# Interleaving the first two MLP products by pair, an end without GpSimd, and adaLN sums in program order, in a hybrid GLA / DeltaNet block

## The chip, the cores and the metric

The kernel runs on one core of a Trainium2 chip. A core has TensorE (PE, with its weight loads shown as PEld), VectorE (DVE), ScalarE (ACT), GpSimd (POOL) and SyncE (SP). Each engine works through its own instructions in order, and semaphores join the engines. Data lie in HBM, in SBUF (128 partitions) and in PSUM, where TensorE writes its results. Most transfers are issued by SP, in the order of its queue, and some by ACT.

The metric is the time of one execution on the device, in microseconds (us). The profile is of one execution; its span runs from the first to the last instruction.

## The reference

One residual block for a sequence of 1024 tokens and a model width of 1024, all in float32. `c` is a conditioning vector. In short:

```
mod = silu(c) @ ada_w + ada_b                 # 6 x 1024: shift1 scale1 gate1 shift2 scale2 gate2
h   = rms_norm(x, pre_mix_w) * (1 + scale1) + shift1
proj = h @ w_in                               # q, k, v, gates of both branches
o_a = gla_chunked(...)                        # gated linear attention, 4 heads, chunks of 64
o_d = gated_delta_chunked(...)                # gated delta rule, 8 heads, chunks of 64
merged = sigmoid(m_a) * (o_a @ w_branch_gla) + sigmoid(m_d) * (o_d @ w_branch_gdn)
x  = x + gate1 * rms_norm(merged @ w_out, post_mix_w)
h2 = rms_norm(x, pre_mlp_w) * (1 + scale2) + shift2
y  = square(relu(h2 @ mlp_w1)) @ mlp_w2       # D_FF = 4096
x  = x + gate2 * rms_norm(y, post_mlp_w)
```

The delta branch needs, for each head, a decay matrix `exp(gc_i - gc_j)` below the diagonal, with `gc` the running sum of the log gates.

## The kernel before

**Numbers.** Each matrix product takes three passes: an operand is split into a high part (an ACT cast) and a low part (a DVE subtraction), and high x high, high x low and low x high are summed in PSUM.

**Order of the work.** The first part of the program, up to the `flush()` in line 1250, leaves the order on each engine to a planner, which places instructions by their dependencies, their place in the program and its own estimates of time. `tc.issue_after(ins)` adds an order without a wait: what is traced inside comes later than `ins` on the engine of `ins`. A counter of ticks spreads work along the matrix products: `at(dt, fn)` (line 328) traces `fn` when `dt` more ticks have gone by (an entry that is due runs at the next tick), and `tick()` is called after every group of matmuls (of a dense tile's eight k steps, each one; of a product of the MLP's first layer, two). From line 1254 on, the token stage and the MLP, the class `InOrder` (line 27) chains every instruction of PE, DVE, ACT, POOL and SP behind the one traced before it on that engine: there the order is the program's.

**Stages by time in the profile.** To about 100 us: loads, norms, the first part of adaLN. About 100 to 210 us: the key tiles of the delta branch (`dense_b` in line 395, eight ticks for a tile; `conv` in line 560 reads a tile's PSUM, one ACT pass and three DVE passes; PSUM holds two such tiles). In it `gdn_D` (line 640) loads `gr`, at tick 4 `decay` (line 632) makes eight DVE instructions and an exponential of it, at tick 10 it is stored. Then the branch gates and a triangular solve on DVE, the GLA heads (`gla_head`), the delta heads (`gdn_head`, to about 1100 us), the branch products, and the token stage (eight tiles of 128 tokens: `merged @ w_out`, norm, residual, second norm, transposes `tr`, lines 1279 to 1315), to about 1370 us.

**The rest of adaLN.** Four of the six parts of `mod` are summed on DVE along the GLA and delta heads: `ada_rest(n)` (line 1078), called at tick 2 + 13 n for n from 0 to 31, loads a block `araw` of 128 rows on SP into one of two `sl` buffers, and eight ticks later `ada_sum` (line 1085) adds it to `aacc`. After each eighth, `ada_total` three ticks later (line 1094) sums over the partitions with TensorE and makes the column `gcol` on DVE, and two ticks after that `ada_row` (line 1109) transposes `gcol` on TensorE.

**The MLP.** The two matrix products are done by a Strassen-Winograd scheme with seven products on 2 x 2 blocks. The hidden width is cut into 16 pairs g. *Pass 1* (lines 1475 to 1501) makes for each pair the product with block B11 (12 matmuls into a bank), copies the bank out with ACT (`uy[:, 0]`, stored to `u_d`), then goes on in the same bank with B21 (12 matmuls), and ACT takes relu and square (`uy[:, 1]`, stored to `y_d`). Weights come as `raw`, 512 KB for a pair; `prep_pass1` makes the high and low parts of one product. `t_ops` are the block differences T1 to T4 and their splits (19 steps) for *pass 2*, which does the other five products of each pair (lines 1642 to 1669) with weights from `prep_pass2`. `uy` lies in the two `sl` buffers, which the token stage uses for `xr` just before. Then comes the second layer (line 1736 on), whose last chunk is done token tile by token tile (line 1804 on), each followed by `finish` (line 1767): add the tile to `yacc` on DVE, square sum on ACT, product with the gate on GpSimd, an inverse root on DVE for that tile (13 small instructions), and one tile later a scaling on ACT and the last addition on GpSimd, and the store. In the last tile the halves are done apart.

Of the kernel before, what the change touches and what calls it, by code (L numbers as in the profile page):

```python
# [26 lines left out]
class InOrder:  # L27


    def __init__(self, tc, engine):  # L30
        self.tc, self.engine, self.strict, self.last = tc, engine, False, None

    def __getattr__(self, name):
        fn = getattr(self.engine, name)
        if not self.strict:
            return fn

        def call(*args, **kw):
            with self.tc.issue_after(self.last) if self.last else nullcontext():
                r = fn(*args, **kw)  # L40
            self.last = r.ins
            return r
        return call


@with_exitstack
def block_kernel(ctx: ExitStack, tc: tile.TileContext, x, c, ada_w, ada_b, pre_mix_w, post_mix_w,
# [1030 lines left out]
    def ada_rest(n):  # L1078
# [3 lines left out]
        DMA.dma_start(raw, ada_w[k * 128:(k + 1) * 128, ADA[i][0]:ADA[i][0] + 1024])  # L1082
        at(8, lambda: ada_sum(i, k, raw))

    def ada_sum(i, k, raw):
        if k == 0:
            adat[i] = t4(p="aacc", tag="hd")
            V.tensor_scalar(adat[i], raw, sc[:, k:k + 1], None, ALU.mult)
        else:
            V.scalar_tensor_tensor(adat[i], raw, sc[:, k:k + 1], adat[i], ALU.mult, ALU.add)  # L1090
        if k == 7:
            at(3, lambda: ada_total(i))

    def ada_total(i):
# [4 lines left out]
        if dst is None:  # L1099
# [3 lines left out]
            at(2, lambda: ada_row(i, g))  # L1103
# [175 lines left out]
    def token_chain(t, ps, xr):  # L1279
# [79 lines left out]
    raw1 = {}  # L1359

    def load_pass1(g):

        r_ = rp.tile([128, 8, 2, 128], F32, tag="raw", name=nm("raw"))
        for i in range(2):
            LD.dma_start(r_[:, :, i, :], mlp_w1[:, (g + i) * 256:(g + i) * 256 + 128].rearrange("(k p) c -> p k c", p=128))
            raw1[g + i] = r_[:, :, i, :]
# [14 lines left out]
    for t in range(NT):  # L1381
# [12 lines left out]
        if t == 7:
            prep_pass1(0, 0, 3)
            prep_pass1(0, 1, 4)
            at(6, lambda: split_op("B21", F[0][2:4], (1,)))
# [77 lines left out]
    at(12, lambda: todo.extend(t_ops()))  # L1475
    for g in range(NG):
        ps = pat()
        uy = pair_tile("uy", "sl")
        if g % 2 == 0:
            at(3, lambda g=g: load_pass1(g + 4) if g + 4 < NG else load_pass2((g + 4 - NG) // 2))  # L1480
        if g + 1 < NG:
            if g:
                prep_pass1(g + 1, 0, 0)
            prep_pass1(g + 1, 1, 1)
        if g == NG - 2:
            todo += prep_pass2(0)
        if g == NG - 1:
            load_uy(0)
        for j in (1, 3) if g < NG - 2 else range(4):
            at(j, lambda: some(1))  # L1490
# [6 lines left out]
        def store(g=g, uy=uy):  # L1497
            LD.dma_start(u_d[g], uy[:, 0])
            LD.dma_start(y_d[g // 2][0, :, g % 2, :], uy[:, 1])

        at(2, store)
# [345 lines left out]
```

## Time and profile before

| | us |
|---|---|
| median of 3 runs (2037.9 to 2039.47) | 2039.18 |
| the profiled execution: time | 2040.46 |
| the profiled execution: span | 2038.7 |
| ACT busy in it | 786.3 |
| POOL busy in it | 214.7 |
| mean granted TensorE clock (1 is full) | 0.983 |

The views used below: the *page* has busy times of the engines; the *windows* give busy time, number of instructions and granted clock (PEclk) in stretches of the span; the *waits* say which engine stood for whom (in all, times, longest); the *timeline* has instructions in order of time, merged where they are alike, with the idle time before them in square brackets; the *chain* is the work that ended last, followed back from the end. `<-` stands between what is written and what is read, or between an engine and the one that released it. L40 is the line in `InOrder` that all instructions of the strict part have, so there one goes by the tiles' names. L365 is a dense tile's matmul.

### The profile page before, as it was taken

Reading aid. Unit: us, or ns where it says so; the run is one execution under the profiler, and the core shown is the slowest. Engines: PE = TensorE matmul, PEld = TensorE weight load, DVE = VectorE, ACT = ScalarE, POOL = GpSimd, SP = SyncE. Lnnn points to the kernel's source line nnn. Section 1 sums busy time; section 2 is a strip of 40 time slices with the busy share of each in tenths; the row PEclk is TensorE's granted clock in tenths of the full one; section 3 lists DMA queues with packets and bytes.
Section 4 is the critical chain, followed back from the end, with each engine's and each line's share of the span. In section 5 each row is a group of like instructions: output and inputs, shape, how many; then the busy total and the mean of one; then the engine's idle time right before and its main releaser. Section 6 shows DMA issues by size and latency. Waiting matters only on the chain.

```text
span 2038.7 us, 26028 instructions
## 1 busy us (share of the span) xinstructions
PE 1943.1 (95%) x9894; PEld 1628.7 (80%) x9894; DVE 1469.8 (72%) x2642; ACT 786.3 (39%) x1410; POOL 214.7 (11%) x131
## 2 busy tenths in 40 slices
PE   6999999999899999999999999998899999999995
PEld 4777888989799878888887888876688888888884
DVE  7757699568658697778777455664478886777877
ACT  5544323243242333333434121354544546433332
POOL 4300100310110100000002121000011110000015
PEclk8899999999899999999999999998999999999998
DMA  9356632213211343233435342334567777353334
GB/s 298 114 207 223 215 104 83 94 52 125 62 53 54 105 158 101 91 92 110 132 109 179 123 143 93 107 100 135 165 207 227 242 226 263 136 206 115 133 114 145
DMA packets 198797, 287.52 MB, mean 141 GB/s; under 512 B 33536, under 2 KB 137423, under 8 KB 198671
## 3 DMA queue, kind: packets, MB, share of 16 engines
q1 hardware_dynamic: 176910, 250.84, 37.9%
q10 hardware_dynamic: 21760, 35.01, 4.8%
q8 instruction: 78, 1.28, 0.3%
q14 instruction: 49, 0.39, 0.1%
HBM read 210.70 MB, written 75.11 MB: 140 GB/s over the span
## 4 chain that ended last, share of the span: by engine, by line
PE 70%; DVE 18%; ACT 5%; DMA 5%; issue 2%; SPq 0%; POOL 0%; DVEq 0%; ACTq 0%; POOLq 0%
PE pm L365 30%; PE pa L40 20%; PE pm L40 9%; DVE obT L587 4%; DMA araw<-in_ada_w_dram 2%; DVE rt L40 2%; PE pm L984 1%; DVE cv L564 1%; PE pm L986 1%; PE pm L985 1%; DVE rs L40 1%; DVE wL L351 1%; PE pa L778 1%; ACT uy L40 1%; DVE xr L40 1%
## 5 line engine op out<-in xcount | busy, mean ns | idle before, releaser
L365 PE MATMUL pm<-hH,wH 128*128 128x512 f32 x1008 | 330.4, 408 | 7.1 <-DVE cv L564 7.1
L365 PE MATMUL pm<-hH,wL 128*128 128x512 f32 x1008 | 314.0, 392 | 1.6 <-DVE wL L351 1.6
L365 PE MATMUL pm<-hL,wH 128*128 128x512 f32 x1008 | 314.7, 393 | 0.0
L365 PEld LDWEIGHTS pm<-hH,wL 128*128 128x128 f32 x1008 | 190.1, 189 | 43.8 <-DVE wL L351 2.0
L365 PEld LDWEIGHTS pm<-hL,wH 128*128 128x128 f32 x1008 | 190.5, 189 | 41.7
L40 PE MATMUL pa<-w,yH 128*128 128x512 f32 x688 | 212.0, 389 | 0.0
L350 ACT CAST wH<-raw 128x1024 fp32r<-128x1024 f32 x95 | 99.1, 1052 | 287.9 <-PE pm L365 203.8
L365 PEld LDWEIGHTS pm<-hH,wH 128*128 128x128 f32 x1008 | 177.2, 191 | 33.5 <-issue 5.0
L40 DVE TENSOR_TENSOR w<-raw,w 128x512 fp32r<-128x512 f32 (+1 forms) x142 | 122.1, 873 | 81.9 <-ACT w L40 81.4
L40 PEld LDWEIGHTS pa<-w,yH 128*128 128x128 f32 x688 | 129.1, 188 | 27.1 <-DVE ya L40 0.4
L40 PE MATMUL pa<-oB,w 128*128 128x512 f32 x480 | 120.8, 407 | 19.6 <-ACT uy L40 19.6
L40 PE MATMUL pa<-w,yL 128*128 128x512 f32 x344 | 133.8, 389 | 0.0
L40 ACT CAST w<-raw 128x512 fp32r<-128x512 f32 (+1 forms) x143 | 96.9, 710 | 87.6 <-DVE raw L40 82.3
L40 PEld LDWEIGHTS pa<-oB,w 128*128 128x128 f32 x480 | 92.0, 195 | 45.5 <-ACT uy L40 26.4
L351 POOL TENSOR_TENSOR wL<-raw,wH 128x1024 fp32r<-128x1024 f32 x27 | 66.3, 2459 | 582.3 <-ACT wH L350 562.1
L564 DVE SCALAR_TENSOR_TENSOR cv<-pm,ccol,cv 128x1023 f32<-128x1023 f32 (+2 forms) x72 | 92.1, 1279 | 20.0 <-ACT cv L562 19.1
L351 DVE TENSOR_TENSOR wL<-raw,wH 128x1024 fp32r<-128x1024 f32 x68 | 83.6, 1236 | 27.8 <-ACT wH L350 26.2
L40 PE MATMUL pm<-oT,w 128*128 128x512 f32 x384 | 90.8, 389 | 0.0
L40 PE MATMUL pa<-oT,w 128*128 128x512 f32 x384 | 90.8, 389 | 0.0
L40 DVE TENSOR_TENSOR ya<-pa,ya 128x512 f32<-128x512 f32 x82 | 55.8, 690 | 43.7 <-PE pa L40 43.6
L40 PEld LDWEIGHTS pa<-oT,w 128*128 128x128 f32 x384 | 72.1, 188 | 15.0
L40 PEld LDWEIGHTS pm<-oT,w 128*128 128x128 f32 x384 | 72.1, 188 | 15.0
(368 smaller groups left out, 3932.9 us busy)
## 6 DMA issues: line engine op xcount, KB each, us to landing
yL<-y_d SPq DMA_DIRECT2D x53, 512.0 KB, 8.6
raw<-in_mlp_w_dram SPq DMA_DIRECT2D x24, 1024.0 KB, 5.7
raw<-in_w_in_dram SPq DMA_DIRECT2D x19, 1024.0 KB, 5.3
raw<-in_w_in_dram SPq DMA_DIRECT2D x34, 512.0 KB, 4.5
araw<-in_ada_w_dram SPq DMA_DIRECT2D x32, 512.0 KB, 3.8
araw<-in_ada_w_dram SPq DMA_DIRECT2D x32, 256.0 KB, 6.3
sg_d<-sig ACTq DMA_DIRECT2D x16, 512.0 KB, 6.4
sl<-sg_d SPq DMA_DIRECT2D x16, 512.0 KB, 4.5
```

Of the source, the lines that this page charges most:

```text
L40: r = fn(*args, **kw)
L350: A.copy(wH, raw_ap)
L351: E.tensor_tensor(wL, raw_ap, wH.bitcast(F32), ALU.subtract)
L365: last["pe"] = T.matmul(ps[:, hf * 512:(hf + 1) * 512], wt[:, k, :], rhs(k, hf, lo), start=(k == 0 and wt is wH and lo == 0), stop=(k == 7 ...
L564: last["ev"] = V.scalar_tensor_tensor(y[:, s:], ps[:, :S - s], ccol[:, (3 - s) * 24 + ct:(3 - s) * 24 + ct + 1], y[:, s:], ALU.mult, ALU.a ...
L587: V.transpose(dst[b:b + 32, :, a:a + 32], src[a:a + 32, :, b:b + 32])
L778: T.matmul(pt[:, i * 128:(i + 1) * 128], kT[:, sl], q[:, sl], start=True, stop=True)
L984: T.matmul(pp, hH[k][:, tok], wh[:, k % 4, :], start=(k == 0), stop=False)
L985: T.matmul(pp, hH[k][:, tok], wl[:, k % 4, :], start=False, stop=False)
L986: last["pe"] = T.matmul(pp, hL[k][:, tok], wh[:, k % 4, :], start=False, stop=(k == 7)).ins
```

## The change

- `InOrder` now remembers the last instruction of its engine (`recent`) in the planned part too. `V.behind()` puts what is traced inside it behind the last DVE instruction traced so far. `decay` and `ada_sum` are traced in it. `decay` is due at tick 8 for head 0 (4 for the others), its store at 12.
- The load of `araw` comes behind the last weight load of the program on SP. `ada_total` comes 8 ticks after the last sum (3 before), `ada_row` 10 ticks after that (2 before).
- The transposes `tr` of the token stage come one tick later.
- Pass 1 goes through the products in the order (0,0), (1,0), (0,1), (2,0), (1,1), ...: between the two products of a pair lie the second of the pair before and the first of the pair after. Parts of the weights are made two products ahead. Two fixed buffers hold `raw`, loaded pair by pair. `uy` lies in `w4` buffers for g below 4 and from 10 on, and in the `sl` buffers for the others; its two halves are stored one by one. Pass 2's weights are loaded one pair further ahead, and those of its first two pairs are made within pass 1.
- At the end, `x1` is loaded for all tiles first, the gate product is on DVE, the last scaling and addition are one DVE instruction, and the inverse root is made for two tiles at once up to tile 5 (for 6 and 7 one by one). GpSimd has nothing there.

```diff
     def __getattr__(self, name):
         fn = getattr(self.engine, name)
-        if not self.strict:
-            return fn
         def call(*args, **kw):
-            with self.tc.issue_after(self.last) if self.last else nullcontext():
+            with self.tc.issue_after(self.last) if self.strict and self.last else nullcontext():
                 r = fn(*args, **kw)
-            self.last = r.ins
+            self.recent = r.ins
+            if self.strict:
+                self.last = r.ins
             return r
+    def behind(self):
+        return self.tc.issue_after(self.recent)
...
     def decay(gr, h):
-        with tc.issue_after(last["ev"]):
+        with V.behind():
...
-        at(4, lambda: decay(gr, h))
-        at(10, lambda: ST.dma_start(Dt_d[h], gr))
+        at(4 if h else 8, lambda: decay(gr, h))
+        at(12, lambda: ST.dma_start(Dt_d[h], gr))
...
-        DMA.dma_start(raw, ada_w[k * 128:(k + 1) * 128, ADA[i][0]:ADA[i][0] + 1024])
+        with tc.issue_after(last["dma"]):
+            DMA.dma_start(raw, ada_w[k * 128:(k + 1) * 128, ADA[i][0]:ADA[i][0] + 1024])
         at(8, lambda: ada_sum(i, k, raw))
     def ada_sum(i, k, raw):
+        with V.behind():
...
-            at(3, lambda: ada_total(i))
+            at(8, lambda: ada_total(i))
...
-            at(2, lambda: ada_row(i, g))
+            at(10, lambda: ada_row(i, g))
...
-        at(8, lambda: tr(0))
-        at(9, lambda: tr(1))
+        at(9, lambda: tr(0))
+        at(10, lambda: tr(1))
...
-    for g in range(NG):
-        ps = pat()
-        uy = pair_tile("uy", "sl")
...
-        prod1(ps, w1.pop((g, 0)), "B11", True)
-        A.copy(uy[:, 0], ps)
-        prod1(ps, w1.pop((g, 1)), "B21", False)
-        A.activation(uy[:, 1], ps, AF.Relu)
-        A.activation(uy[:, 1], uy[:, 1], AF.Square)
...
+    PASS1 = [(0, 0)] + [e for g in range(NG - 1) for e in ((g + 1, 0), (g, 1))] + [(NG - 1, 1)]
+    for n, (g, k) in enumerate(PASS1):
+        if n + 2 < len(PASS1):
+            prep_pass1(*PASS1[n + 2], 0)
+        if n % 2 and n // 2 + 4 < NG:
+            at(0, lambda n=n: load_pass1(n // 2 + 4))
...
+        if n < 24:
+            at(0, lambda: some(1))
+            if n % 2:
+                at(1, lambda: some(1))
...
+        if k == 0:
+            acc1[g] = pat()
+            uy1[g] = pair_tile("uy", "sl" if 4 <= g < 10 else "w4")
+            prod1(acc1[g], w1.pop((g, 0)), "B11", True)
+            A.copy(uy1[g][:, 0], acc1[g])
+            store(u_d[g], uy1[g][:, 0])
+        else:
+            prod1(acc1[g], w1.pop((g, 1)), "B21", False)
+            A.activation(uy1[g][:, 1], acc1.pop(g), AF.Relu)
+            A.activation(uy1[g][:, 1], uy1[g][:, 1], AF.Square)
+            store(y_d[g // 2][0, :, g % 2, :], uy1.pop(g)[:, 1])
...
     def finish(t, ps):
-            tt(V if end and not i else G, yg[:, c_], ya[:, c_], gw2[0][:, c_], mul)
+            tt(V, yg[:, c_], ya[:, c_], gw2[0][:, c_], mul)
+            if end and not i:
+                last_scale()
...
+    def scale(t):
+        if t < 6 and t % 2 == 0:
+            return
+        n = 2 if t < 6 else 1
...
+        r = rsqrt(v, n)
+        if t == NT - 2:
+            fin["r6"] = r
+            return
+        for j in range(n):
+            u = t - n + 1 + j
+            for i, c_ in enumerate(HALF if t == NT - 1 else [FULL]):
+                V.scalar_tensor_tensor(xrs[u][:, c_], fin[u][:, c_], r[:, j:j + 1], xrs[u][:, c_], ALU.mult, ALU.add)
+                (ST if i else LD).dma_start(out[u * 128:(u + 1) * 128, c_], xrs[u][:, c_])
```

More of the change, by code (lines that the diff above doesn't have):

```diff
@@ L1357, in w_low @@
         tt(V, w[:, 1], src, w[:, 0].bitcast(F32), sub)
-    raw1 = {}
+    raw1, ring = {}, []
     def load_pass1(g):
[L1363 to L1366, printed above, removed]
+        if len(ring) < 2 and g % 2 == 0:
+            ring.append(rp.tile([128, 2, 8, 128], F32, tag="raw", name=nm("raw")))
+        raw1[g] = ring[g % 4 // 2][:, g % 2]
+        LD.dma_start(raw1[g], mlp_w1[:, g * 256:g * 256 + 128].rearrange("(k p) c -> p k c", p=128))
     w1 = {}
@@ L1440, in block_kernel, with load_pass2 @@
     raw2 = {}
-    def load_pass2(g):
-        r_ = raw2[g] = rp.tile([128, 8, 256], F32, tag="raw", name=nm("raw"))
-        LD.dma_start(r_, mlp_w1[:, g * 256:(g + 1) * 256].rearrange("(k p) c -> p k c", p=128))
+    def load_pass2(g, parts=None):
+        parts = parts or (rp.tile([128, 8, 256], F32, tag="raw", name=nm("raw")),)
+        n = 8 // len(parts)
+        raw2[g] = [parts[k // n][:, k % n:k % n + 4] for k in (0, 4)]
+        for i, r_ in enumerate(parts):
+            LD.dma_start(r_, mlp_w1[i * n * 128:(i + 1) * n * 128, g * 256:(g + 1) * 256].rearrange("(k p) c -> p k c", p=128))
     w2p = {}
@@ L1450, in prep_pass2 @@
         raw = raw2[g]
-        q = {(i, k): raw[:, 4 * k:4 * k + 4, i * 128:(i + 1) * 128] for i in range(2) for k in range(2)}
+        q = {(i, k): raw[k][:, :, i * 128:(i + 1) * 128] for i in range(2) for k in range(2)}
         def high(key, src):
@@ L1473, in load_uy @@
         LD.dma_start(uy[:, 1], y_d[g // 2][0, :, g % 2, :])
[L1475 to L1501 removed]
+    at(13, lambda: todo.extend(t_ops()))
@@ L1643, in block_kernel @@
     banks_of(0)
-    ahead2 = prep_pass2(1)
-    for j in range(4):
-        at(j, ahead2.pop(0))
+    ahead2 = p1
     product1(0, "P6")
@@ L1774, in finish @@
             tt(V, ya[:, c_], ps[i] if end else ps, ya[:, c_], add)
-            A.activation(jk[:, c_], ya[:, c_], AF.Square, accum_out=v2[:, i:i + 1])
-        for i, c_ in enumerate(parts):
-            tt(V if end and not i else G, yg[:, c_], ya[:, c_], gw2[0][:, c_], mul)
-        while post:
-            post.pop()()
-        v = small(1, "cv")
-        if end:
-            V.tensor_add(v, v2[:, 0:1], v2[:, 1:2])
-        V.tensor_scalar(v, v if end else v2[:, 0:1], 1.0 / D, EPS, ALU.mult, ALU.add)
@@ L1784, in finish @@
-        r = rsqrt(v, 1)
-        def scale():
-            if t == NT - 2:
-                V.scalar_tensor_tensor(xr, yg, r, xr, ALU.mult, ALU.add)
-            else:
-                A.activation(yg, yg, AF.Copy, scale=r)
-                tt(G, xr, xr, yg, add)
-            LD.dma_start(out[t * 128:(t + 1) * 128, :], xr)
-        if not end:
-            post.append(scale)
-        else:
-            for i, c_ in enumerate(parts):
-                V.scalar_tensor_tensor(xr[:, c_], yg[:, c_], r, xr[:, c_], ALU.mult, ALU.add)
-                (ST if i else LD).dma_start(out[t * 128:(t + 1) * 128, c_], xr[:, c_])
+            A.activation(jk[:, c_], ya[:, c_], AF.Square, accum_out=fin["v"][:, j:j + 1])
@@ L1802, in block_kernel @@
     YS = {(0, 0): 0, (0, 1): 1, (1, 0): 3, (1, 1): 2}
     flush()
+    for t in range(NT):
+        xrs.append(t4(p="xr"))
+        LD.dma_start(xrs[t], x1_d[t])
     for t in range(NT):
```

64 lines of the change are left out of this document (46 added, 18 removed).

## The prediction

> **What bounds the kernel now.** I read the page first, then the windows by stage, then what TensorE waits for, then the timeline at each of those waits.
>
> ```profile
> PE 1943.1 (95%) x9894; PEld 1628.7 (80%) x9894; DVE 1469.8 (72%) x2642; ACT 786.3 (39%) x1410; POOL 214.7 (11%) x131
> ```
>
> TensorE is busy for 1943.1 of 2038.7 us, and no matmul is added or taken away. So the change can only win what TensorE stands idle (95.6 us) and what it loses to a lower clock. Where that lies (stretch, busy PE PEld DVE ACT POOL, granted clock, DMA share, GB/s):
>
> ```profile
> 210.00:534.00 324.00, 324.00 (x1770) 279.32 (x1768) 248.75 (x538) 112.84 (x155) 37.02 (x20) 1.00 0.32 104
> 1370.14:1487.91 117.77, 98.19 (x400) 75.58 (x398) 55.58 (x91) 62.07 (x110) 0.00 (x0) 0.96 0.47 150
> 1487.91:1972.31 484.40, 484.40 (x2138) 400.82 (x2136) 383.80 (x461) 217.13 (x295) 36.31 (x28) 1.00 0.57 192
> 1972.31:2038.70 66.39, 44.04 (x193) 35.70 (x191) 47.96 (x121) 15.64 (x24) 32.47 (x14) 0.87 0.32 111
> ```
>
> From 210 to 534 us and in all of pass 2 and the second layer TensorE never stands; nothing can be won there. Pass 1 (the second row) loses some 20 us, and the end (the last row) has 22 us without TensorE. The waits name the rest (in all, times, longest):
>
> ```profile
> PE pa L40 <- ACT uy L40: 19.6, 16, 3.6
> ...
> PE pa L1111 <- DVE gcol L1102: 8.6, 2, 7.5
> PE pm L365 <- DVE cv L564: 7.1, 2, 4.4
> ```
>
> **Part 1: the column `gcol`.** `ada_row` is traced two ticks after `ada_total`, and TensorE, in order, stands until DVE has come to the column:
>
> ```profile
> 541.78 0.38 PE L1111 MATMUL pa<-ident,gcol 128*8 128x128 f32 x1 [7.49 <-DVE gcol L1102]
> ```
> ```profile
> 540.00:545.00 5.00, 3.22 (x9) 0.50 0.28 109
> 545.00:550.00 5.00, 5.00 (x19) 0.77 0.00 0
> ```
>
> The wait is 8.6 us in its two instances. After the long one the clock is at 0.50 and 0.77: 3.22 x 0.50 + 5.00 x 0.23 = 2.8 us more. Ten ticks instead of two give DVE eight ticks more, each six matmuls, that is some 11 us; DVE was 7.5 us late. So the whole is won: **11.4 us**. What could be late next is the sum before it, which has eight ticks too. If DVE were over 13 us late, the remainder would come back.
>
> **Part 2: sums that the planner moved ahead.** The program calls `ada_rest` only from the GLA heads on, but the sums run from 177 us, among the key tiles:
>
> ```profile
> L1090 DVE SCALAR_TENSOR_TENSOR aacc<-araw,sc,aacc x28: 1275/1282/1287, 177.3 to 1114.5; 128x1024 f32<-128x1024 f32 x28
> ```
> ```profile
> 181.15 1.28 DVE L1090 SCALAR_TENSOR_TENSOR aacc<-araw,sc,aacc 128x1024 f32<-128x1024 f32 x1 [2.57 <-DMA araw<-in_ada_w_dram]
> 188.48 0.80 PE L365 MATMUL pm<-hH,wH 128*128 128x512 f32 x2 [4.36 <-DVE cv L564]
> ```
> ```profile
> 180.00:190.00 10.00, 5.64 (x28) 0.95 0.99 311
> 190.00:200.00 10.00, 9.54 (x47) 0.88 0.64 221
> ```
>
> ```profile
> PE pm L365 <- DVE wL L351: 1.6, 1, 1.6
> ```
>
> One waits 2.57 us for its transfer with the convolution's passes behind it on DVE, others lie between those passes, and TensorE stands 4.36 us for the bank. A low part of a weight is late by 1.6 us soon after. `V.behind()` makes this place impossible, as the last DVE instruction traced then is one of the GLA head. Won: 4.36 + 1.6, and by the clock 5.64 x 0.05 + 9.54 x 0.12 = 1.4: **7.4 us**. The sums (1.28 us each, 32 of them) then lie evenly, one in 13 ticks (some 18 us), and add 7% to DVE. In 210 to 534 us DVE is busy for 248.75 of 324 us and TensorE never stands, which is the cover. In the delta heads DVE is busier, and TensorE's small waits there can become shorter or longer: 0, between -4 and +4 us.
>
> The other wait of `cv` is the decay's:
>
> ```profile
> 111.66 2.19 DVE L636 SCALAR_TENSOR_TENSOR gr<-gr,gcC,negmask 128x128 f32<-128x128 f32 x8 [4.74 <-DMA gr<-gc_d]
> 115.19 0.71 PE L365 MATMUL pm<-hH,wH 128*128 128x512 f32 x2 [2.75 <-DVE cv L564]
> ```
>
> DVE waits 4.74 us for `gr` between two passes of a convolution. For head 0 the new tick 8 still comes ahead of that convolution in the program, and `behind` only sets a lower bound. I expect it to stay where it is: **0 us**, at best 2.75.
>
> **Part 3: transposes one tick later, and pass 1.**
>
> ```profile
> L40 PE MATMUL pa<-ident,xh 128*128 128x128 f32 x64 | 9.8, 275 | 2.5 <-DVE xh L40 2.5
> ```
> ```profile
> 1754.63 65.28 PE pa L40 x288
> ```
>
> Six transposes wait 2.5 us in all (0.4 each); a tick of six matmuls covers that: **2.5 us** won. The second row gives the pace of such matmuls without waits: 65.28 / 288 = 0.227 us, so 2.72 us for a product of 12. Pass 1 has 32 products: 87.0 us, and 16 of the transposes lie in it (16 x 9.8 / 64 = 2.4 us, an upper bound, as they overlap). The stretch takes 117.77, so 28 us are there to be won, waits and slow clock together. One steady period of before, from a pair's relu to the next product:
>
> ```profile
> 1414.94 0.60 ACT L40 ACTIVATE uy<-pa 128x512 f32<-128x512 f32 x1 [3.11 <-PE pa L40]
> 1415.57 0.63 ACT L40 ACTIVATE uy<-uy 128x512 f32<-128x512 f32 x1
> 1416.11 1.12 ACT L40 CAST w<-raw 128x512 fp32r<-128x512 f32 x2
> ...
> 1416.74 0.69 DVE L40 TENSOR_TENSOR w<-raw,w 128x512 fp32r<-128x512 f32 x1 [2.85 <-ACT w L40]
> 1417.14 1.04 ACT L40 CAST oT<-F 128x1024 fp32r<-128x1024 f32 x1
> 1417.35 1.22 DVE L40 TENSOR_TENSOR F<-F,F 128x1024 f32<-128x1024 f32 x1
> 1418.09 0.58 ACT L40 COPY uy<-pa 128x512 f32<-128x512 f32 x1
> ```
> ```profile
> 1418.72 5.74 PE L40 MATMUL pa<-oB,w 128*128 128x512 f32 x24 [1.09 <-ACT uy L40]
> ```
>
> TensorE stands because the second product goes into the bank that ACT must first copy out, behind two weight casts and one of T's. With two foreign products (5.44 us) between, the copy has that long. ACT's work for a pair is 0.58 + 0.60 + 0.63 + 1.12, and 1.5 casts of T (1.6): 4.5 of 5.44 us. DVE's is two low parts (1.4) and 3 steps with 2.8 instructions of 1.22 (3.4): 4.8. Both fit, but not by much. What is late next:
>
> - *The first products.* Behind the last token tile comes ACT's square sum (1.3 us; a cast of that size takes 1.04), then on DVE a product (1.2), 13 small instructions (2.3, below) and a scaling (1.28), and only then the low part for the third product (0.7): 6.8 us after the tile's end. TensorE wants it after two products, at 5.4, or with eight transposes at 6.6. I take 0.7 us, between 0 and 3.
> - *The `sl` buffers.* For g from 6 to 9 the copy needs the buffer of g - 2, whose last store is issued only after that pair's relu.
>
> ```profile
> DMA to landing us min/median/max: 2.0/3.7/6.2
> ```
>
> This is for `u_d`; for `y_d` no row shows it. Copy 0.58, a weight cast 0.56, casts of T 0.8, relu and square 1.23, issue 0.3 and the landing form a loop: 5.5 us at 2.0, 7.2 at 3.7, 9.7 at 6.2, against 5.44 of TensorE. Over four turns it falls 0, 7 or 17 us behind, of which about 4 are covered, as parts are made two products ahead. That costs 0, 3 or 13 us; I take 1, near the lower rows, since a `y` store goes behind one load, where before a `u` store often went behind two.
>
> So pass 1 takes 87.0 + 2.4 + 0.7 + 1.0 = 91.1 us: **26.7 us** won. Pass 2's loads come a pair earlier, which DVE hides now; 0. The new loads and stores are as many bytes as before (0.47 of DMA in the second window row).
>
> **Part 4: the end.**
>
> ```profile
> 2020.31 1.22 DVE L40 TENSOR_TENSOR ya<-pm,ya 128x1024 f32<-128x1024 f32 x1
> 2023.97 2.34 POOL L40 TENSOR_TENSOR xr<-xr,yg 128x1024 f32<-128x1024 f32 x1
> 2024.07 2.27 DVE L40 TENSOR_TENSOR rt<-rt,cv 128x1 f32<-128x1 f32 x1
> 2031.61 0.15 DVE L40 TENSOR_TENSOR cv<-fv 128x1 f32<-128x1 f32 x1
> ```
> ```profile
> 2034.10 1.41 DVE L40 SCALAR_TENSOR_TENSOR xr<-yg,rs,xr 128x512 f32<-128x512 f32 x2
> 2035.55 0.38 ACTq L1800 DMA_DIRECT2D out_dram<-xr  x1
> ```
>
> DVE sets the pace now: beside GpSimd's 2.34 us instruction an instruction of 128 x 1 lasts 2.27 us. The 14 small ones from 2031.61 to 2034.10, with GpSimd idle, take 2.5 us together. After the change DVE has for two tiles 2 x (1.22 + 1.22), a chain of 13 (2.3) and 2 x 1.28: 9.7 us, and about 0.4 of waits for ACT's square sum, against 48 matmuls, 10.9 us. So TensorE sets the pace to tile 5. Counting from 1972.31, tile k ends at 5.44 (k + 1). The second scaling of tiles 4 and 5 ends on DVE about 40.2; then tile 6's two products (2.3, its bank is ready since 38.1), a wait of 0.3, its chain (2.3): 45.1; tile 7's halves with tile 6's scaling between them (0.6 + 0.6 + 1.2 + 0.6 + 0.6) and a wait of 0.3: 49.0; 14 small ones 2.5; two scalings 1.4: 52.9; issue and landing of the last store as now (2038.7 - 2035.51 = 3.2): 56.1. I take 57, for gaps between instructions. 66.39 - 57 = **9.4 us** won, between 8 and 10.5. The loads of `x1`, eight of 512 KB ahead of the stores on SP, are needed from 16 us on, in turn; at 192 GB/s (third window row) one takes 2.7 us, so they are hidden.
>
> **Sum.** 11.4 + 7.4 + 0 + 2.5 + 26.7 + 9.4 = 57.4 us. The profiled execution took 2040.46, 1.3 above the median; less 57.4 it is 1983.1, and the median 2039.18 becomes **1981.8 us**.
>
> **Rivals.**
> - *ACT is held by the `sl` buffers.* At a landing of 6.2 us pass 1 costs 12 us more than I took: 1994. For it: a load of 512 KB stands ahead of each `y` store on SP. Against: only four turns, and slack afterwards. Chance 0.12.
> - *The order isn't what it says.* `behind` is a lower bound; the planner may put sums and decay among other passes, with the waits of part 2 or new ones in the delta heads of that size: 7 us lost, 1989. Chance 0.14.
> - *Slower: sums in order stand for their transfers.* Each load of `araw` comes behind the last weight load on SP, and such loads wait long:
>
> ```profile
> SPq L171 <- DVE wL L351: 380.2, 39, 36.7
> ```
>
>   If SP stood 10 us after the time at which the load should go, the sum, now fixed on DVE, would hold what is behind it. It decides from 57.4 / 32 = 1.8 us of TensorE's time for each sum on: at 2.5 us it gives 2062. Against: SP waits there because it runs ahead (the mean is 9.7 us while TensorE never stands from 210 to 534 us), and the sum has eight ticks. Chance 0.03.
> - *Slower: the clock falls in the interleaved pass.* If changing banks with every product made small gaps, and the clock stayed at the 0.50 of part 1, 32 products would cost 87 us more: 2069. [...] Against it stands the third window row: pass 2 changes banks after 12 or 24 matmuls for 484.40 us at clock 1.00. Chance 0.01.
>
> **How the numbers follow.** The forecast (all four parts, each within its bounds: 1974 to 1988) has 0.66; 0.04 are left for more than that, if the decay's wait and the heads' small waits go too (1972). The range takes in the first two rivals up to 1995: **1972 to 1995**, with about 0.12 outside. Under 0.2% (4 us) a measurement can't tell a change from none. Faster 0.95, same 0.01, slower 0.04.
>
> **What would show it.** Right: no wait of TensorE for `gcol`; no `aacc` before the GLA heads; pass 1 at about 91 us with hardly a wait for `uy`; no GpSimd after the second layer, small DVE instructions at 0.16 us, an end of about 57 us. Wrong: TensorE waiting for `w` or ACT for a `y_d` store in the middle of pass 1; `cv` waits at 188 us still there; DVE standing for `araw`.

## The result and the profile after

| | before | after |
|---|---|---|
| median, us (runs) | 2039.33 (2037.9 to 2039.64, 4) | 1975.22 (1974.3 to 1985.12, 4) |
| profiled execution: time, span | 2040.46, 2038.7 | 1974.3, 1972.6 |
| its TensorE clock | 0.983 | 0.993 |

The ratio is 0.9698, 95% interval [0.9667, 0.9729]: faster by 3.0%. The forecast was 1981.8 us, in a range of 1972 to 1995. In the records of the changed kernel every operation that goes through `InOrder.call` has line L38, so groups are told apart by their tiles. The page's busy times of the changed kernel:

```profile
PE 1924.5 (98%) x9894; PEld 1621.9 (82%) x9894; DVE 1467.7 (74%) x2617; ACT 779.5 (40%) x1404; POOL 189.5 (10%) x117
```

TensorE does the same 9894 matmuls and stands for 48.1 us in place of 95.6. The windows by stage of the changed kernel, cut where the same matmul starts in every kernel below (stretch, length, then busy PE, PEld, DVE, ACT, POOL, granted clock, DMA share, GB/s): start, key tiles to solve, GLA, delta heads, za and od, token tiles, pass 1, pass 2 with the second layer, end.

```profile
0.00:73.99 73.99, 52.88 (x249) 41.51 (x250) 57.46 (x116) 40.33 (x54) 31.74 (x29) 0.88 0.71 218
73.99:351.68 277.69, 274.53 (x1296) 228.12 (x1294) 219.74 (x429) 111.66 (x234) 25.18 (x15) 0.99 0.47 155
351.68:588.77 237.09, 237.09 (x1540) 212.35 (x1539) 164.35 (x367) 88.67 (x152) 33.33 (x21) 1.00 0.27 87
588.77:1078.81 490.04, 480.80 (x2884) 413.73 (x2883) 395.70 (x736) 179.38 (x404) 21.59 (x12) 1.00 0.38 118
1078.81:1252.02 173.21, 173.21 (x796) 144.17 (x795) 95.10 (x115) 31.24 (x53) 36.01 (x15) 1.00 0.38 128
1252.02:1339.26 87.24, 87.24 (x410) 72.28 (x408) 57.28 (x213) 40.53 (x84) 0.00 (x0) 1.00 0.32 109
1339.26:1432.41 93.15, 90.62 (x401) 73.12 (x400) 57.81 (x92) 63.48 (x113) 0.00 (x0) 1.00 0.59 191
1432.41:1916.85 484.44, 484.44 (x2138) 400.82 (x2136) 378.84 (x458) 214.67 (x293) 41.62 (x28) 1.00 0.56 198
1916.85:1972.60 55.75, 43.68 (x193) 35.85 (x191) 41.45 (x96) 9.51 (x18) 0.00 (x0) 0.93 0.20 77
```

Before, the same stretches took 75.3, 288.4, 247.3, 493.4, 174.5, 91.2, 117.8, 484.4 and 66.4 us, so they gained 1.3, 10.7, 10.3, 3.4, 1.3, 4.0, 24.6, 0.0 and 10.6 us: 66.1 in all, 8.7 more than forecast. Two of these rows of before, key tiles and GLA:

```profile
75.32:363.68 288.36, 276.14 (x1296) 228.58 (x1294) 226.34 (x443) 113.17 (x235) 24.82 (x15) 0.99 0.49 161
363.68:611.02 247.34, 239.85 (x1541) 214.24 (x1539) 159.62 (x359) 88.14 (x151) 32.59 (x21) 0.98 0.24 79
```

The waits of TensorE that matter here, of those left from the key tiles to the second layer (in all, times, longest):

```profile
PE pa L38 <- DVE t L38: 5.2, 4, 1.9
...
PE pa L38 <- DVE cv L38: 2.6, 1, 2.6
PE pa L38 <- ACT w L38: 2.5, 2, 1.4
...
PE pm L38 <- DVE cv L38: 0.5, 1, 0.5
```

No row for `gcol`, `uy` or `xh` is there; new is a wait of 2.5 us for `w`, in pass 1.

### The profile page after: what moved, and what is told of

The parts are those of the page before. It is cut to its first block, busy times and chain, and to the rows that moved or that the text cites. A ratio compares the mean times of both kernels' runs of the same rounds, so it can differ in the third digit from the quotient of the medians.

```text
span 1972.6 us, 25955 instructions
## 1 busy us (share of the span) xinstructions
PE 1924.5 (98%) x9894; PEld 1621.9 (82%) x9894; DVE 1467.7 (74%) x2617; ACT 779.5 (40%) x1404; POOL 189.5 (10%) x117
## 4 chain that ended last, share of the span: by engine, by line
PE 85%; DVE 10%; DMA 3%; ACT 2%; issue 1%; SPq 0%; DVEq 0%; ACTq 0%
PE pm L38 55%; PE pa L38 30%; DVE obT L38 2%; DVE cv L38 1%; DMA araw<-in_ada_w_dram 1%; DVE si L38 1%; DVE acc L38 1%; DVE t L38 1%; DVE rt L38 0%; DMA x<-in_x_dram 0%; ACT ob L38 0%; DMA dec_d<-dec 0%; DVE sqt L38 0%; DVE sqr L38 0%; DMA gr<-gc_d 0%
## 5 line engine op out<-in xcount | busy, mean ns | idle before, releaser
L38 PE MATMUL pm<-hH,wH 128*128 128x512 f32 x1008 | 327.6, 405 | 0.5 <-DVE cv L38 0.5
L38 PE MATMUL pm<-hL,wH 128*128 128x512 f32 x1008 | 314.3, 392 | 0.0
L38 PE MATMUL pm<-hH,wL 128*128 128x512 f32 x1008 | 312.2, 391 | 0.1
L38 PEld LDWEIGHTS pm<-hH,wL 128*128 128x128 f32 x1008 | 189.4, 188 | 42.0 <-DVE wL L38 0.5
L38 PEld LDWEIGHTS pm<-hL,wH 128*128 128x128 f32 x1008 | 189.5, 188 | 41.3
L38 PE MATMUL pa<-w,yH 128*128 128x512 f32 x688 | 212.1, 389 | 0.0
L38 ACT CAST wH<-raw 128x1024 fp32r<-128x1024 f32 x95 | 99.0, 1051 | 284.3 <-PE pm L38 205.2
L38 PEld LDWEIGHTS pm<-hH,wH 128*128 128x128 f32 x1008 | 176.2, 189 | 26.7 <-issue 1.1
L38 DVE TENSOR_TENSOR w<-raw,w 128x512 fp32r<-128x512 f32 (+1 forms) x142 | 123.3, 872 | 52.4 <-ACT w L38 51.4
L38 PEld LDWEIGHTS pa<-w,yH 128*128 128x128 f32 x688 | 129.0, 188 | 27.2 <-DVE ya L38 0.4
L38 PE MATMUL pa<-w,yL 128*128 128x512 f32 x344 | 133.8, 389 | 0.0
L38 ACT CAST w<-raw 128x512 fp32r<-128x512 f32 (+1 forms) x143 | 98.2, 709 | 88.4 <-DVE raw L38 79.2
L38 POOL TENSOR_TENSOR wL<-raw,wH 128x1024 fp32r<-128x1024 f32 x27 | 66.1, 2453 | 570.0 <-ACT wH L38 551.0
L38 PE MATMUL pa<-oB,w 128*128 128x512 f32 x480 | 113.1, 392 | 2.5 <-ACT w L38 2.5
L38 DVE SCALAR_TENSOR_TENSOR cv<-pm,ccol,cv 128x1023 f32<-128x1023 f32 (+2 forms) x72 | 92.1, 1280 | 22.1 <-ACT cv L38 20.9
L38 PEld LDWEIGHTS pa<-oB,w 128*128 128x128 f32 x480 | 89.2, 188 | 23.3 <-ACT w L38 3.8
L38 DVE TENSOR_TENSOR wL<-raw,wH 128x1024 fp32r<-128x1024 f32 x68 | 83.6, 1236 | 27.3 <-ACT wH L38 27.0
L38 PE MATMUL pm<-oT,w 128*128 128x512 f32 x384 | 90.8, 389 | 0.0
L38 PE MATMUL pa<-oT,w 128*128 128x512 f32 x384 | 90.8, 389 | 0.0
L38 DVE TENSOR_TENSOR ya<-pa,ya 128x512 f32<-128x512 f32 x82 | 55.9, 690 | 43.7 <-PE pa L38 43.7
L38 PEld LDWEIGHTS pm<-oT,w 128*128 128x128 f32 x384 | 72.1, 188 | 15.0
L38 PEld LDWEIGHTS pa<-oT,w 128*128 128x128 f32 x384 | 72.1, 188 | 15.0
```

## The experiments

Each kernel below is the changed one with one edit, unless it says otherwise. A stage's length is read from its own profile. In two profiles of the changed kernel the stages repeat to 0.1 us, but for three: start (74.0 and 75.3 us), key tiles (277.7 and 281.5) and delta heads (490.0 and 494.8), of which more below.

**Ticks of the columns** (`u_cols`).

```
-            at(8, lambda: ada_total(i))
+            at(3, lambda: ada_total(i))
...
-            at(10, lambda: ada_row(i, g))
+            at(2, lambda: ada_row(i, g))
```

> The changed kernel with the two ticks put back: ada_total three ticks after the last sum, ada_row two ticks after ada_total. Everything else as changed. My theory (part 1): the waits of TensorE for gcol and the slow clock behind them are what the later ticks removed, so they return: 8.6 us of waits in two instances and 2.8 us by the clock, 11.4 us in all, nearly all of it in the GLA stretch (237.1 us now, 247 to 249 then); the time goes from 1974.3 to about 1985.7. Rival: the sums lie in program order now, so DVE is not late with them any more and the old ticks would do; then TensorE waits under 2 us for gcol and the time stays within 3 us of 1974.3.

Measured: 1989.92 us (1988.8 to 1994.52). The GLA stretch and TensorE's longest new wait, in windows and timeline:

```profile
351.82:597.17 245.35, 241.64 (x1541) 215.81 (x1539) 164.24 (x367) 88.63 (x152) 33.34 (x21) 0.98 0.26 84
```
```profile
521.60 1.63 PE L38 MATMUL pa<-onesR,aacc 128*128 128x1 f32 x7 [3.71 <-DVE aacc L38]
```

GLA lost 8.3 us, za and od 2.5: 10.8, near the 11.4 expected; the rival falls. The heads took 4.0 more, but with 494.1 us they lie within what they vary by without an edit. The wait came back, but one step earlier in the chain: for the sum `aacc` (5.7 us in three instances) more than for `gcol` (1.4). The rest of GLA's loss is the same work taking longer, at a clock of 0.98 and not 1.00. The two ticks were put back together; what each is worth alone was not tried.

**Order of the adaLN sums** (`u_sums`, and each half of it alone).

```
-        with tc.issue_after(last["dma"]):
-            DMA.dma_start(raw, ...)
+        DMA.dma_start(raw, ...)
...
-        with V.behind():
+        with nullcontext():
```

> The changed kernel with the order of the adaLN sums undone in both places: the loads of araw are not held behind the last weight load, the sums not behind the last DVE instruction; the later ticks stay. My theory (part 2): sums move back among the key tiles, TensorE waits there again for cv and wL, 4.36 + 1.6 us and 1.4 us by the clock: the stretch of key tiles, gates and solve, 277.7 us now, takes 285 us. It took 11.2 us less after the change, not 7.4; if all of that is the sums' doing, it takes 289. The start (74.2 now) may go back to 75.6, as two loads of araw are issued at 45 us again ahead of weights. Time 1982 to 1987. Rival: what gained in the key tiles was the decay's place, not the sums; then 280.5 at most, and the time under 1978.

Measured: 1989.19 us (1986.57 to 1991.77); the key stretch in the windows and the two waits:

```profile
74.56:363.48 288.92, 278.91 (x1295) 231.48 (x1294) 231.99 (x449) 112.44 (x235) 24.11 (x15) 0.98 0.49 160
```
```profile
PE pm L38 <- DVE cv L38: 3.9, 2, 3.5
PE pm L38 <- DVE wL L38: 3.5, 1, 3.5
```

DVE does 20 instructions more in this stretch, TensorE waits for exactly the two things named in part 2, and the stretch is 11.2 us longer than in the changed kernel (0.6 more than before the change): TensorE stands 6.9 us more (10.0 in place of 3.2), and its work takes 4.4 us more, at a clock of 0.98 and not 0.99.

The loads' order alone undone (`u_dma`):

> The changed kernel without the order of the loads alone: loads of araw may go ahead of weight loads on SP, while each sum stays behind the last DVE instruction. Theory A: the place of the sums on DVE is what matters; the key stretch stays at 277.7 us within 1.5, only the start loses its 1.4 us again, and the time is 1974.3 to 1977. Theory B: early loads of 512 KB delay weights and the decay's transfer: TensorE waits 2.75 us again for the decay in the key tiles, and the time is 1978 or more.

Measured: 1982.48, 1983.67, 1984.58 and once 1974.97 us; profiled: key stretch 281.6, heads 495.2. By its numbers this is theory B. But the instructions of TensorE, DVE, ScalarE and GpSimd stand in the same order in this program as in the changed kernel, GLA stays at 237.1 us, and one execution ran at the changed kernel's time. That put the question of `again` below.

The order on DVE alone undone (`u_vb`):

> The changed kernel without the order of the sums on DVE alone: the loads of araw stay behind the last weight load. Theory A (the order on DVE is what counts, the loads do not matter): sums are put ahead again, now into places where their transfers are later still, so DVE stands for araw and the stretch of key tiles takes 285 us or more; time 1982 or more. Theory B (the loads' order pulls the sums along, since a sum is not put ahead of its load): no sum before the GLA heads, every stretch within 1.5 us of the changed kernel, time within 3 us of 1974.3.

Measured: 1981.4 us (1980.73 to 1981.9), key stretch 280.1 (with the decay's wait of `again` below, 3.1 us), GLA 241.5. Neither theory as it stands: the loads' order keeps the sums out of the key tiles (no 285 us), but five of them come ahead among the GLA heads, and TensorE waits there for DVE:

```profile
387.07 0.37 PE L38 MATMUL pa<-zm,ks 128*64 128x64 f32 x1 [1.94 <-DVE ks L38]
```

So the loads' order alone is not enough. The order on DVE alone is: with it (`u_dma`) no sum moves, and no run shows a gain that is due to the loads' order.

**The decay** (`u_decay`).

```
-        with V.behind():
+        with tc.issue_after(last["ev"]):
...
-        at(4 if h else 8, lambda: decay(gr, h))
-        at(12, lambda: ST.dma_start(Dt_d[h], gr))
+        at(4, lambda: decay(gr, h))
+        at(10, lambda: ST.dma_start(Dt_d[h], gr))
```

> The changed kernel with the decay's part undone: its instructions held behind the last eviction and not behind the last DVE instruction, tick 4 for head 0 too, its store at tick 10. In the changed kernel the decay of head 0 still stands between two passes of a convolution on DVE; its transfer had landed there, so TensorE waits 0.45 us instead of 2.75. Theory A (transfer): the transfer of gr lands late when the store of dec, in packets of 4 bytes, is issued ahead of it on ScalarE's queue (0.9 us ahead in the kernel before and in two of the runs that undid one thing, 0.2 to 0.4 us behind it in the others); the edit decides nothing by itself. Then the key stretch takes 277.7 us where dec is stored behind, 280 to 282 where it is stored ahead, and the trace shows which. Theory B (the edit): tick and order are what removed the wait; then DVE waits over 2 us for gr again although dec is stored behind it, or the decay comes ahead of the conv pass and another wait takes its place.

Measured: 1982.25 us (1980.76 to 1983.39), key stretch 282.1. `dec` (64 numbers that the delta heads need, spread to `decB` by a store and a load) was stored at 100.69 us. The load of `gr` for head 0 goes at about 100.25 us, an estimate: `gc_d`, which it reads, was stored at 98.37 us, and in `again` the load goes 1.88 us after that store. So `dec` was stored behind it, theory A forecast 277.7, and it is not that. The timeline shows the wait one head on:

```profile
106.84 3.33 DVE L38 SCALAR_TENSOR_TENSOR gr<-gr,gcC,negmask 128x128 f32<-128x128 f32 x8
114.97 2.19 DVE L38 SCALAR_TENSOR_TENSOR gr<-gr,gcC,negmask 128x128 f32<-128x128 f32 x8 [3.60 <-DMA gr<-gc_d]
118.94 1.12 PE L38 MATMUL pa<-ident,cv 128*128 128x128 f32 x4 [3.11 <-DVE cv L38]
```

Head 0's transfer is there in time; the decay of head 1, one place earlier on DVE without the edit, waits for its own, and TensorE waits behind it. Why that transfer is late, SP's queue shows:

```profile
108.21 0.33 SPq L544 DMA_DIRECT2D decB<-dec_d  x1
108.59 1.37 SPq L646 DMA_DIRECT2D gr<-gc_d  x3
```

The load of `decB` reads what the store of `dec`, issued at 100.69, writes; it went 7.5 us after that store, and the loads of `gr` for heads 1 to 3 stand behind it. So both count where `dec` is stored behind: head 0's transfer is in time by itself, and head 1 needs the edit, which is worth 4.4 us there (282.1 against 277.7; tick and order were not tried singly).

**The changed kernel once more** (`again`, no edit).

> The changed kernel itself, once more, as the kernel to compare with. One kernel that differs from it in the order of loads on SP alone had an execution of 1974.97 us among three of 1982.5 to 1984.6, so two paces of one program are to be expected here too: some executions at 1974 to 1977 us and some at 1982 to 1986. Theory A (chance in the start): which of the two it is hangs on whether TensorE's clock falls at 84 us after a wait of 2.6 us, which delays ScalarE and so puts the store of dec behind the load of gr; a profile with that cold stretch has a key stretch of 277.7 us, one without it 280 to 282. Theory B: the loads' order is what the 4 us hang on; then this kernel stays at 277.7 in the profile and at 1974 to 1977 in nearly all executions.

Measured: 1984.2, 1975.81, 1980.21, 1980.43 and 1974.3 us; with the first four, nine executions of one program from 1974.3 to 1985.1, median 1976.14. The profiled one took 1984.2: key stretch 281.5, heads 494.8, every other stretch from GLA on within 0.1 us of the first profile. Theory A holds for the two profiles; but the executions do not fall into its two paces, as two of five took 1980 us. The timeline, the changed kernel's first profile in the first fence, the second in the next:

```profile
84.73 1.05 PE L38 MATMUL pa<-ident,cv 128*128 128x128 f32 x4
99.25 0.36 SPq L646 DMA_DIRECT2D gr<-gc_d  x1
99.66 0.48 ACTq L542 DMA_DIRECT2D dec_d<-dec  x1
105.81 3.34 DVE L38 SCALAR_TENSOR_TENSOR gr<-gr,gcC,negmask 128x128 f32<-128x128 f32 x8
```
```profile
85.62 0.60 PE L38 MATMUL pa<-ident,cv 128*128 128x128 f32 x4
99.37 0.47 ACTq L542 DMA_DIRECT2D dec_d<-dec  x1
100.33 0.36 SPq L646 DMA_DIRECT2D gr<-gc_d  x1
110.88 2.19 DVE L38 SCALAR_TENSOR_TENSOR gr<-gr,gcC,negmask 128x128 f32<-128x128 f32 x8 [5.27 <-DMA gr<-gc_d]
114.40 1.19 PE L38 MATMUL pm<-hH,wH 128*128 128x512 f32 x2 [3.27 <-DVE cv L38]
```

In the first profile four transposes run at half clock (1.05 us in place of 0.60). From their start to the store of `dec` it takes 14.9 us in the first and 13.8 in the second; ScalarE, which works on TensorE's output there, is later in the first. So `dec`, 0.2 KB in 80 packets (by so many SP's queue has more in `f_all` below, where the store goes there), is stored 0.4 us behind the load of `gr` in the one and 1.0 us ahead of it in the other, and then DVE stands 5.27 us for `gr`. The windows show the slow load: from 100 to 105 us 13 GB/s in all in `u_dma`, where the store is 0.93 us ahead and DVE stands 5.14 us for `gr`, and 139 GB/s in the first profile. A half clock at 84 us (four transposes in 1.05 to 1.06 us) and the store behind (0.2 to 0.4 us) go together in three profiles (the first, `u_cols`, `u_sums`), and so do full clock (0.60 us) and the store ahead (0.9 to 1.1 us) in three (the second, `u_dma`, `u_vb`), with a wait of TensorE of 3.1 to 3.3 us behind head 0's decay. No run sets the clock, so that it decides the order is read from these profiles alone. It holds for the changed program's order only: the kernel before has slow clock there too (0.60 in the window from 83.8 to 87.2 us), and yet stores `dec` 0.85 us ahead. The clock in the window from 83.8 to 87.2 us, first and second profile:

```profile
83.80:87.20 3.40, 3.40 (x11) 2.73 (x11) 3.25 (x4) 3.28 (x15) 1.91 (x1) 0.50 0.21 86
```
```profile
83.80:87.20 3.40, 3.40 (x19) 2.89 (x20) 3.24 (x5) 2.77 (x13) 0.62 (x1) 1.00 0.38 154
```

The heads differ by the clock alone: TensorE is busy for 480.8 and 485.5 us with the same 2884 matmuls, at a clock of 1.00 and 0.99, and stands 9.2 us in both. One wait of 1.86 us in the timeline and the window of 6.83 us behind it, first profile and then second:

```profile
722.47 1.14 PE L38 MATMUL pa<-t,a 64*64 64x64 f32 x16 [1.86 <-DVE t L38]
```
```profile
722.47:729.30 6.83, 6.83 (x56) 5.77 (x57) 5.71 (x10) 2.64 (x3) 0.00 (x0) 1.00 0.48 135
```
```profile
727.57 1.64 PE L38 MATMUL pa<-t,a 64*64 64x64 f32 x13 [1.86 <-DVE t L38]
```
```profile
727.57:734.40 6.83, 6.83 (x32) 6.04 (x33) 3.54 (x8) 2.06 (x2) 0.00 (x0) 0.50 0.41 123
```

The same wait cost nothing more in the one and 3.4 us (half of 6.83) in the other.

**Transposes one tick earlier** (`u_tr`: `at(8, ...)`, `at(9, ...)` for `tr`).

> The changed kernel with the transposes of the token tiles back at ticks 8 and 9. My theory (part 3): six transposes wait 0.4 us each for xh again, 2.5 us; the token stretch goes from 87.2 to 89.7 us. The stretch took 4.0 us less after the change, so if the rest (four transposes that now lie in pass 1, 0.6 to 0.9 us, and what the pipeline needs to fill again behind each wait) is the tick's doing too, it goes to 91.2, and pass 1 gains up to 0.9 back. Rival: the tiles' chains run otherwise now, since the casts for pass 1 lie elsewhere, and the old ticks would do: token stretch 87.2 within 0.5.

Measured: 1988.71 us (1984.33 to 1990.27), token stretch 91.3, pass 1 94.2. The wait:

```profile
PE pa L38 <- DVE xh L38: 2.6, 6, 0.5
```

The tick is worth 4.1 us there: 2.6 of waits, as forecast, and 1.5 of busy time. Part of that is four transposes which in the changed kernel lie behind the stretch (408 weight loads in place of 412); the remainder was not taken apart. Pass 1 does not give it back, it takes 1.1 us more as well. The rest of the profiled execution's 10 us lies in the start, the key tiles and the heads, where the edit does nothing; the other executions have no profile.

**Pass 1 as before** (`u_pass1`: `load_pass1` by two, `prep_pass1` one pair ahead, both products of a pair into one bank in succession, pass 2's loop as before).

> The changed kernel with the loops of pass 1 and pass 2 as before: both products of a pair one after the other into one bank, parts made one pair ahead, raw weights loaded by two pairs, and t_ops at tick 12. My theory (part 3): the whole gain of pass 1 is the order of its products; the stretch goes from 93.2 to 117.8 us within 2, by waits for uy of 1 us in each pair, and slow clock of up to 5 us; pass 2 with the second layer stays at 484.4; time 1998 to 2000. Rival: the interleaving moved part of the cost into the token stretch or pass 2, or the decay-free clock hides part of it; then pass 1 rises by less than 20 us, or another stretch falls by over 2 us.

Measured: 2007.19 us (2003.78 to 2010.84), and in windows and waits

```profile
1350.10:1467.55 117.45, 98.71 (x402) 76.04 (x401) 54.74 (x89) 62.40 (x110) 0.00 (x0) 0.96 0.47 150
1467.55:1951.96 484.41, 484.41 (x2138) 400.82 (x2136) 383.57 (x461) 217.72 (x295) 36.14 (x28) 1.00 0.58 198
```
```profile
PE pa L38 <- ACT uy L38: 18.7, 16, 2.6
```

All 24.3 us hang on this part, nothing of it was moved elsewhere. The time is above the 1998 to 2000 us expected: start, key tiles and heads, which the edit does not touch, took 1.9, 4.1 and 4.9 us more in this profile than in the changed kernel's first.

**The end, piece by piece** (`e_norm1`, `e_gate`, `e_add`). The edits: a chain for each tile; `tt(V if end else G, yg, ...)`; for tiles 0 to 5 `A.activation(yg, yg, AF.Copy, scale=r)` and `tt(G, xr, xr, yg, add)`.

> The changed kernel with the norms of the end tile by tile and not by two tiles; products, gains and sums stay on DVE, GpSimd stays out. My theory (part 4): GpSimd beside DVE's small instructions was the larger part, the pairing pays for what DVE then has to do besides: a tile costs DVE 1.22 + 1.22 + 0.2 (wait) + 2.3 + 1.28 = 6.2 us against 5.44 of TensorE, so tile 5 ends some 2.9 us later on DVE, and the end goes from 55.7 to 58.6 us, of the 66.4 of before. Rival: the pairing is the larger part: the end goes to 61 or more, as each single norm stands for ScalarE's square sum (1.06 + 0.2 us) with nothing to fill the wait. Second rival: TensorE hides the tiles all the same and the end stays under 56.5.

> The changed kernel with one instruction of each tile of the end but the last back on GpSimd: the product with the gain, yg. Norms stay by two tiles, sums on DVE. My theory (part 4): beside GpSimd's 2.4 us instruction one small instruction of DVE's chain takes 2.3 us and not 0.16; DVE has 1.22 us less for each tile but that stall once for two tiles and a wait for ScalarE's square sum (1.2 us) that yg filled; that hides to tile 5, and the tail with tile 6 is 1 to 2 us longer: the end goes from 55.7 to 57 or 58 us. Rival: the load taken from DVE is worth more than the stall: the end gets shorter, to 54 or 55 us.

> The changed kernel with the other instruction of the end back on GpSimd: for tiles 0 to 5 ScalarE scales yg (about 1.1 us) and GpSimd adds it to x1 (2.4 us), as in the kernel before; norms by two tiles and the gain's product on DVE stay. Singly undone, the pairing cost 1.6 us and the gain's product on GpSimd 1.8 us of the 10.7 us that the end gained, so either this sum is the largest piece, or the pieces cover each other. Theory A (the sum is the piece): small instructions of the chains of tiles 5 and 6 last 2.3 us beside it; the end goes from 55.7 to 59 us or more. Theory B (they cover each other): with pairs the two sums (4.8 us) lie between two chains, DVE is rid of 2.5 us for a pair and stalls once, in tile 6's chain; the end stays between 54.5 and 57.5 us, and what set the old end was that both products stood on GpSimd in every tile, so that each chain met one.

Measured, the end's window of each in this order (medians 1980.22, 1980.31 and 1979.9 us):

```profile
1917.76:1975.10 57.34, 43.68 (x193) 35.85 (x191) 47.04 (x135) 9.53 (x18) 0.00 (x0) 0.91 0.19 75
```
```profile
1923.40:1980.90 57.50, 43.68 (x193) 35.86 (x191) 36.97 (x89) 9.51 (x18) 16.78 (x7) 0.91 0.19 75
```
```profile
1923.35:1980.60 57.25, 43.68 (x193) 35.85 (x191) 41.01 (x90) 15.74 (x24) 17.23 (x6) 0.91 0.19 75
```

The pieces cover each other: each alone undone costs 1.5 to 1.8 us, while the whole part, which also loads `x1` ahead, won 10.6. My 2.9 us for the single norms was too much; the rivals of the first two fall, theory B of the third holds.

**A version that goes further** (`f_all`).

```
-            ST.dma_start(dec_d.rearrange("(r u) -> r u", u=1), dec)
...
-        DMA.dma_start(decB, dec_d.partition_broadcast(128))
...
-        DMA.dma_start(gr, gc_d[h].partition_broadcast(128))
+        ld = DMA.dma_start(gr, gc_d[h].partition_broadcast(128)).ins
+        if h == 3:
+            with tc.issue_after(ld), nc.allow_non_contiguous_dma(reason="tiny"):
+                DMA.dma_start(dec_d.rearrange("(r u) -> r u", u=1), decs["dec"])
+            DMA.dma_start(decB, dec_d.partition_broadcast(128))
...
-            at(0, lambda n=n: load_pass1(n // 2 + 4))
+            at(3, lambda n=n: load_pass1(n // 2 + 4))
...
-        if t < 6 and t % 2 == 0:
-            return
-        n = 2 if t < 6 else 1
+        if t % 2 == 0:
+            return
+        n = 2
```

> The changed kernel with three edits in three stretches. (1) The store of dec and the load of decB on SP behind the load of gr for head 3, so that 64 packets of 4 bytes cannot stand ahead of the first load of gr: if that is what made gr late, the key stretch is 277.7 us or less in every profile, with or without the cold stretch at 84 us, and the kernel's executions spread less; if gr is late for another reason, 280 to 282 comes as often as before. (2) In pass 1 each load of weights three ticks later, behind the store of y on SP: if that store's landing (4.4 to 5.0 us after its issue) is what held ScalarE's copy three times and TensorE 2.5 us for w, pass 1 goes from 93.2 to 90.7 us; if the landing is as long without a load ahead, it stays within 0.5. (3) The norms of tiles 6 and 7 in one chain: DVE has one chain of 2.1 us less behind the last products, and the end goes from 55.7 to 53.7 us; if TensorE or ScalarE's square sum sets the end and not DVE, it stays within 0.5. In all 1970 us where all three hold, 1974 where none does.

Measured: 1968.62 us (1967.19 to 1970.3), ratio to before 0.9648 [0.9635, 0.9661]; `again`, on the same chip, 0.9692 [0.9678, 0.9705]. Key stretch, pass 1 and end in the windows, and the decay's row:

```profile
74.60:350.16 275.56, 272.86 (x1296) 226.99 (x1294) 220.76 (x429) 111.35 (x234) 25.18 (x15) 1.00 0.49 156
1340.95:1429.93 88.98, 88.98 (x401) 73.62 (x400) 57.80 (x92) 63.68 (x113) 0.00 (x0) 1.00 0.64 200
1914.33:1968.60 54.27, 43.69 (x193) 35.85 (x191) 39.64 (x83) 9.51 (x18) 0.00 (x0) 0.94 0.20 79
```
```profile
104.30 3.35 DVE L38 SCALAR_TENSOR_TENSOR gr<-gr,gcC,negmask 128x128 f32<-128x128 f32 x8
```

All three hold. The clock was full at 84 us in this execution (four transposes in 0.60 us), and yet `gr` was there: the load is in time with full clock too, once the store is gone from ahead of it. There is one profile of this kernel, so a half clock at 84 us was not seen with it. The loads of `gr` for heads 1 to 3 no longer stand behind `decB` either. The four executions spread over 3.1 us, the nine of the changed kernel over 10.8. Pass 1 lost its last wait (88.98 us, all busy; 4.2 us and not the 2.5 expected), the end 1.5 us of the 2.0 expected.

## Why the prediction held, step by step

- *Part 1, 11.4 us.* The waits for `gcol` went, and GLA with za and od gained 11.5. That the sum would be late next was named; with the ticks put back (`u_cols`) it is the sum that TensorE waits for most.
- *Part 2, sums, 7.4 us.* Right in place and mechanism: no wait of `cv` at 188 us, and no `aacc` before the GLA heads (the first instruction of the four sums comes at 364.9 us):

```profile
L38 DVE SCALAR_TENSOR_TENSOR aacc<-araw,sc,aacc x28: 1267/1279/1286, 383.9 to 1113.5; 128x1024 f32<-128x1024 f32 x28
```

  In the second profile, where the decay's wait is still there (3.3 us, 2.75 before), the stage gained 6.9 us, in the first 10.7. Undone it costs 11.2 us in that execution, by the same two waits and slow clock (0.98 in place of 0.99). The slower rival (DVE standing for `araw`) did not occur. Of the two orders in the change only the one on DVE is shown to matter.
- *Part 2, decay, "0, at best 2.75".* Head 0's decay stays where it is, as forecast. Whether its `gr` is late was not the edit's doing but that of a store that I had not looked at: 2.3 us of wait in one profile, nothing in the other. Head 1 was overlooked: where head 0 is in time, the wait would come one head later without the edit (`u_decay`, 4.4 us).
- *Part 2, heads, 0 between -4 and +4.* TensorE stands there 9.2 us in both profiles of the changed kernel, against 9.4 before. The stretch went from 493.4 to 490.0 or to 494.8; between the last two only the clock differs.
- *Part 3, transposes, 2.5 us.* 2.6 of waits; mis-sized by the 1.5 us of busy time that went with them.
- *Part 3, pass 1, 26.7 us.* The mechanism was right, but 24.6 us were won, 2.1 less. The 89.4 us of matmuls and transposes were right (`f_all`: 88.98 without a wait). The term of 1.0 for the `sl` buffers was too small: TensorE stood 2.5 us for `w` in the middle, the sign of being wrong that the forecast had named. That of 0.7 for the first products was not needed. ScalarE's copy stood three times for a `y` store, 9.2 us in all:

```profile
1379.30 0.32 SPq L38 DMA_DIRECT2D y_d<-uy  x1
```
```profile
1383.69 0.59 ACT L38 COPY uy<-pa 128x512 f32<-128x512 f32 x1 [2.96 <-DMA y_d<-uy]
```

  That is 4.4 us from issue to copy, with a load of 512 KB ahead on SP. With the load behind it (`f_all`) it is 2.4 (1374.30 to 1376.74), and pass 1 is 4.2 us shorter. This is the first rival, at a third of its 12 us.
- *Part 4, 9.4 us.* 10.6; the 0.9 us kept for gaps between instructions were not needed. `e_norm1`, `e_gate` and `e_add` show that no one piece carries it, as the sum by DVE's time for two tiles had it.
- *The rival of the falling clock.* Pass 1 changes its bank with every product and keeps a clock of 1.00 (the seventh window row); `f_all` does so too, with TensorE busy for all of its 88.98 us.
- *The sum.* 66.1 us against 57.4 in the first profile; in the second, of the same program, 2040.46 - 1984.2 = 56.3. The two differ by 3.8 us in the key tiles, 4.7 in the heads and 1.3 in the start, with the same instructions: more than the 8.7 us by which the forecast was short. Of these 8.7 us, 8.0 lie in those three stages (1.3 in the start and 3.4 in the heads, where the forecast had 0, and 3.3 in the key tiles); transposes and end gave 2.7 more, pass 1 took back 2.1. So which side of the forecast an execution falls on is luck, and the first profile, at its lower bound of 1974, was a lucky one. What the forecast lacked was this: it took the waits and the slow clock of one execution as fixed prices, where they change from one execution to the next.

## What to carry to other kernels

Give an in-order engine its consumer some ticks later than the producer needs, and then look for what is late next in that chain; here it was the sum ahead of the column. Look at each queue for what stands ahead of a transfer that someone waits for: here a load of 512 KB (4.4 us from a store's issue to the copy that needs it, and 2.4 with the load behind) or a store of 0.2 KB (DVE stood 5.27 us for the load behind it) was enough. Before a stretch's gain or loss is put down to an edit, profile the same program twice: two executions here differed by 10 us without any edit.

## What the runs showed of the hardware

- The half clock at 84 us lasted 3.4 us in the first profile of the changed kernel: the window from 83.8 to 87.2 us has 0.50, that from 82.0 to 83.8 us 1.00 and that from 87.2 to 88.9 us 0.99. In the second profile a window of 6.83 us in the heads has 0.50. The waits ahead of them do not tell: TensorE's wait of 2.6 us at 84 us has half clock behind it in the first profile and full clock in the second, and with that of 1.86 us in the heads it is the other way round. What decides it was not shown.
- Beside a GpSimd instruction one DVE instruction took longer and another did not. In `e_add`, while GpSimd adds two tiles in SBUF, DVE's sum with a PSUM operand takes 1.22 us (1.23 in `e_gate` at 1929.04 us, with GpSimd idle), and its product of two SBUF operands takes 3.01 us in place of 1.23:

```profile
1951.53 5.76 POOL L38 TENSOR_TENSOR xr<-xr,yg 128x1024 f32<-128x1024 f32 x2 [5.19 <-PE pm L38]
1952.01 3.01 DVE L38 TENSOR_TENSOR yg<-ya,gw 128x1024 f32<-128x1024 f32 x1
1956.19 1.22 DVE L38 TENSOR_TENSOR ya<-pm,ya 128x1024 f32<-128x1024 f32 x1 [1.17 <-PE pm L38]
```

  In `e_gate` a small instruction with one input (128x2) took 1.38 us beside GpSimd's product, where its like takes 0.17. What in an instruction decides whether it takes longer was not shown.
